# RWKV-7 chain of a two-layer hybrid block: one PSUM tile per pair for U and the state sums, the block product's four copies on ScalarE

## The chip, the cores and the metric

The kernel runs as one program on 1 core of a Trainium2 chip. The metric is the device time of one execution in microseconds (us); the time of a kernel is the median of its runs. One execution was also profiled, and all rows below come from it.

## What is computed

The reference is a two-layer block of a generator. 256 context tokens and 256 latent tokens of width 1024 go through adaLN and RMSNorm, one wide input projection, three bidirectional mixers (mLSTM, RG-LRU, RWKV-7), a gated merge, an output projection and a SwiGLU. The change concerns the RWKV-7 mixer, whose recurrence per head (16 heads of 64) and direction is:

```
def step(s, x_t):
    r_t, w_t, k_t, v_t, kap_t, kapa_t = x_t
    s_kap = jnp.einsum('bhvk,bhk->bhv', s, kap_t)
    s = s * w_t[:, :, None, :] - s_kap[..., None] * kapa_t[:, :, None, :] + v_t[..., None] * k_t[:, :, None, :]
    return s, jnp.einsum('bhvk,bhk->bhv', s, r_t)
```

## The kernel before

All large products are fp32 split into a high and a low part, three matmuls for each 128-row block, 128x512 outputs in layer 0. In each of the two layers a first stage (`weave`) runs five tasks at once: the preparation of the RWKV units (`rw_prep`, `rw_tok`, `rw_solve32` in layer 0, `rw_solve16` in layer 1), the chain (`rw_chain`), the gate of that branch, and a long list of input products (`products`, 1776 matmuls in each layer, the "products" below, tile `mm`). A second stage follows with the mLSTM heads and the RG-LRU (`ml_gates`, `ml_head`, `lru`) and the merge gates' products (line 425, also tile `mm`), then the merge, the output projection and the SwiGLU.

The order of the first stage is written out by the kernel itself when it is built. `weave` keeps a clock of its own, each task yields costs (`op("V", 290)` books 290 ns on VectorE, `took` books matmuls on TensorE, `wait` a fixed delay), and whichever task is due comes next; products are put in where no other task is due or where the recent columns are few. Inside the stage each engine executes exactly that order. The second stage is ordered by the tile scheduler. TensorE, VectorE and ScalarE run their queues strictly in the order given, so an instruction that waits holds up all behind it.

A unit is two pairs of heads (index j) times one half of the tokens; there are 8 units a layer, 8 steps of 32 tokens in each, 128 steps in all. A step (lines 1097 to 1168) is: matmuls of the old state into x (`xy`), a VectorE copy of it (`xs`, line 1106), the scaled old state (`sd`, line 1110), the matmuls for U, four copies of U into the tile UV (lines 1133 and 1136: pair j = 0 on VectorE, j = 1 on ScalarE), the matmuls of the state sums (U and V against k), the new state `Sn` (line 1153, or 1151 in a first step), and the outputs `y` (line 1163 or 1165). The next step's first matmuls wait for `Sn`. The PSUM tile `u2` is two banks of 128x512: pair j has its U in columns 0 to 127 and its state sums in columns 128 to 255 of bank j.

```
u2 = self.two()
us, sp = (u2[:, :, 128 * a:128 * a + 128].rearrange("p j (d v) -> p j d v", v=64) for a in range(2))
...
if j:
    SC.copy(UV[j][b, :, i], us[b, j])
    self.op("S", 256)
else:
    V.tensor_copy(UV[j][b, :, i], us[b, j])
    self.op("V", 290)
```

The program that the tile framework makes of this puts waits between instructions that use the same PSUM tile from two engines. `rw_solve16` (layer 1 only) inverts 32x32 triangles as two 16x16 blocks and a block product: POOL eliminates, DMAs bring the inverses back as `PT` and into `Am`, TensorE forms the two small products (tile `sm`, 16x32 and 32x16 matmuls), ScalarE writes `Z` between them, and four copies (lines 1014 and 1016, two on each engine) put the result into `Am`. The chain of a unit starts when its solve is done. `low_gemm` and `ml_head` use the same two banks outside of the first stage.

Of the kernel before, what the change touches and what calls it, by code (L numbers as in the profile page):

```python
# [22 lines left out]
S = 256  # L23
T = 512
# [189 lines left out]
class KB:  # L214
# [29 lines left out]
    def sm(self, shape):  # L244
        return self.psum("sm", shape, 2)

    def two(self):

        return self.psum("u2", [128, 2, T], 1)

    def tr(self, out, x, ident, hd):

# [303 lines left out]
        return self.pw.tile([128, T], F32, name="stage", tag="stage", bufs=SB)  # L556

    def low_gemm(self, l, h, hooks=None, mid=None, raws=None):
        ps = self.two()
        pss = [ps[:, 0], ps[:, 1]]  # L560
        self.gemm2(pss, [(l, BLK[n]) for n in ("dd", "ad")], h, hooks=hooks, mid=mid, raws=raws)
        return pss

# [397 lines left out]
    def rw_solve16(self, l, u, Am, sc1):  # L961


        nc, V, G, SC, re = self.nc, self.nc.vector, self.nc.gpsimd, self.nc.scalar, self.re
        if u:
            yield ("until", ("solve", l, u - 1))
        yield ("wait", DMW)
        N = re.tile([128, 16, 16], F32, name="N")
        nc.sync.dma_start(out=N, in_=sc1.rearrange("k x h q s t -> (k x h q) s t"))
        yield ("wait", DML)  # L970
        et = re.tile([128, 64], F32, name="et")
        for i in range(1, 15):
            w = 15 - i
            tv = et[:, 0:i * w].rearrange("p (a b) -> p a b", b=w)
            G.tensor_tensor(out=tv, in0=N[:, 0:i, i:i + 1].broadcast_to([128, i, w]), in1=N[:, i:i + 1, i + 1:16].broadcast_to([128, i, w]), op=ALU.mult)
            yield ("on", self.op("G", 280 + 2.3 * i * w) - 1500)
            G.tensor_tensor(out=N[:, 0:i, i + 1:16], in0=N[:, 0:i, i + 1:16], in1=tv, op=ALU.subtract)
            yield ("on", self.op("G", 340 + 2.1 * i * w) - 1500)
        G.memset(N.rearrange("p s t -> p (s t)")[:, 0:256:17], -1.0)
        NT = re.tile([64, 16, 16], F32, name="NT")  # L980
        G.tensor_copy(NT, N[0:64].rearrange("p s t -> p t s"))
        yield ("on", self.op("G", 900) + LAT)
        sc2 = self.dr.tile([3, 2, 2, 16, 16, 16], F32, name="sc2")
        nc.sync.dma_start(out=sc2[0:2].rearrange("k x h q s t -> (k x h q) s t"), in_=N)
        nc.sync.dma_start(out=sc2[2].rearrange("x h q s t -> (x h q) s t"), in_=NT)
        yield ("wait", DML)
        PT = re.tile([128, 16, 16], F32, name="PT")
        HJ = [(x, j, 64 * x + 32 - 32 * j) for x in range(2) for j in range(2)]
        for x, j, b in HJ:
            nc.sync.dma_start(out=PT[b:b + 16], in_=sc2[2, x, j].rearrange("q s t -> s q t"))  # L990
            for k in range(2):
                r = slice(b + 16 * k, b + 16 * k + 16)
                nc.sync.dma_start(out=Am[r, j, :, :, 16 * k:16 * k + 16].rearrange("p d c t -> p (d c) t"), in_=sc2[k, x, j].rearrange("q s t -> s q t"))
        yield ("wait", DMR)

        yield ("lock", "sm")
        ps = self.sm([128, 16, 16])
        for c in range(16):
            for x, j, b in HJ:
                self.mmul(ps[b:b + 32, c], Am[b:b + 16, j, c // 8, c % 8, 0:32], PT[b:b + 16, c])  # L1000
        yield self.took()
        Z = re.tile([128, 16, 16], F32, name="Z")
        SC.activation(out=Z, in_=ps, func=AF.Identity, scale=self.c["odd"])
        yield self.end("S", 420)
        ps = self.sm([128, 16, 16])
        for c in range(16):
            for x, j, b in HJ:
                self.mmul(ps[b:b + 16, c], Z[b:b + 32, c], Am[b:b + 32, j, c // 8, c % 8, 16:32])
        yield self.took()
        for x, j, b in HJ:  # L1010
            o = Am[b:b + 16, j, :, :, 16:32]
            p = ps[b:b + 16].rearrange("p (d c) t -> p d c t", d=2)
            if j:
                SC.copy(o, p)
            else:
                V.tensor_copy(o, p)
            self.op("VS"[j], 420)
        self.locks.discard("sm")
        self.ready[u] = max(self.free[e] for e in "VS") + LAT
        self.done.add(("solve", l, u))  # L1020

    def rw_solve32(self, l, u, Am, sc1):
# [28 lines left out]
    def rw_chain(self, l, n, ctx_out, emit):  # L1051
# [18 lines left out]
        def X(hd, j):  # L1070
            return R[hd ^ j]


        def U(hd, j):
            b = 64 * (hd ^ j) + 32 - 32 * j
            return slice(b, b + 32)
# [20 lines left out]
        for i in range(8):  # L1097
            last = s == 1 and i == 7
            y = None
            if Sp is not None:  # L1100
                for d in range(2):
                    for hd, j in HJ:
                        self.mmul(x[U(hd, j), d], kr[R[hd], j, d, i, 0:32], Sp[R[hd], j, d], start=False, stop=d == 1)
                yield self.took()
            xs = rl.tile([128, 2, 64], F32, name="xs", bufs=2)
            V.tensor_copy(xs, x)
            t = self.op("V", 288)
            if not last and Sp is not None:
                sd = rl.tile([128, 2, 2, 64], F32, name="sd")
                V.tensor_tensor(out=sd, in0=Sp, in1=PL[:, :, :, i].broadcast_to([128, 2, 2, 64]), op=ALU.mult)  # L1110
                self.op("V", 527)
            if yo:
                if "sc" in self.locks:
                    yield ("lock", "sc")
                self.locks.add("sc")
                y = self.psum("sc", [128, 2, 64], 1)
                if Sp is not None:
                    for d in range(2):
                        for hd, j in HJ:
                            self.mmul(y[Q(hd, j), d], kr[R[hd], j, d, i, 32:64], Sp[R[hd], j, d], start=d == 0, stop=False)  # L1120
                    yield self.took(0.0)
            yield ("at", t + LAT)

            u2 = self.two()
            us, sp = (u2[:, :, 128 * a:128 * a + 128].rearrange("p j (d v) -> p j d v", v=64) for a in range(2))
            for d in range(2):
                for hd, j in HJ:
                    self.mmul(us[U(hd, j), j, d], Am[U(hd, j), j, d, i, 0:32], xs[U(hd, j), d])
            yield self.took()
            for hd, j in HJ:  # L1130
                b = U(hd, j)
                if j:
                    SC.copy(UV[j][b, :, i], us[b, j])  # L1133
                    self.op("S", 256)
                else:
                    V.tensor_copy(UV[j][b, :, i], us[b, j])  # L1136
                    self.op("V", 290)
            if i < 7:
                x = tokens(i + 1)
                yield self.took(0.0)  # L1140
            yield ("at", max(self.free[e] for e in "VS") + LAT)
            Sn = None
            if not last:
                for d in range(2):
                    for j in range(2):
                        for hd in range(2):
                            self.mmul(sp[R[hd], j, d], bkT[X(hd, j), j, d, i], UV[j][X(hd, j), d, i], quads=True)
                yield self.took()
                Sn = rl.tile([128, 2, 2, 64], F32, name="Sn", bufs=2)
                if Sp is None:  # L1150
                    V.tensor_copy(Sn, sp)
                else:
                    V.tensor_tensor(out=Sn, in0=sp, in1=sd, op=ALU.add)
            snt = self.op("V", 424) + LAT
            if yo:
                for d in range(2):
                    for hd, j in HJ:
                        self.mmul(y[Q(hd, j), d], Am[X(hd, j), j, d, i, 32:64], UV[j][X(hd, j), d, i], start=Sp is None, stop=Sp is None or d == 1)
                yield self.took()

                o = Y[:, i:8 - i:7 - 2 * i] if i < 4 else (Y[:, i:6 - i:7 - 2 * i] if i < 7 else Y[:, ::-7])
                if i < 4:
                    V.tensor_copy(o, y)
                else:
                    V.tensor_tensor(out=o, in0=y, in1=o, op=ALU.add)
                self.op("V", 282)
                self.locks.discard("sc")
            yield ("at", snt)
            Sp = Sn
# [331 lines left out]
    def ml_head(self, l, hd, src, ctx_out, yd):  # L1501
# [39 lines left out]
                P[d][sb] = W  # L1541
        src = [[[0], [0, 1], [0, 1, 2], [0, 1, 2, 3]], [[0, 1], [1], [0, 1, 2, 3], [0, 1, 3]]]
        u2 = self.two()
        yp = [self.psum("xy", [128, T], 1), u2[:, 0]]
        for tb in range(t0 // 128, 4):
            num = []
            rd = m2.tile([128, 4], F32, name="rd")
            for d in range(2):
                ps = self.psum("sc", [128, 257], 1) if d else u2[:, 1, 0:257]
                lst = src[d][tb]  # L1550
                for n, sb in enumerate(lst):
                    nc.tensor.matmul(ps, P[d][sb][:, 128 * tb:128 * tb + 128], v[:, sb], start=n == 0, stop=n == len(lst) - 1)  # L1552
# [377 lines left out]
```

## Time and profile before

| | before |
|---|---|
| median of 3 runs | 2903.18 us (2895.85 to 2903.63) |
| the profiled execution | 2907.76 us, its span 2906.0 us |
| busy: PE, PEld, DVE, ACT, POOL | 92%, 71%, 60%, 44%, 21% of the span |
| mean granted TensorE clock | 0.96 |
| chain stage, layer 0 and layer 1 (first to last U matmul) | 236.4 to 760, 1871.0 to 2366 us |

PE is the matmul queue, PEld the weight loads beside it, DVE is VectorE, ACT ScalarE, SP the queue that issues most DMAs. Matmuls of the trace overlap, since their ends are modelled: two neighbours that start 0.23 us apart are each shown as 0.39 us long. A bracket behind a row gives the idle time of its engine just before and what ended it. "Issue" means that the profile shows no one that was waited for.

### The profile page before, as it was taken

What the parts mean: (1) busy time and instruction counts of PE and PEld (TensorE: products, weight loads), DVE (VectorE), ACT (ScalarE), POOL (GpSimd) and SP (SyncE); (2) the same over time, 40 slices, a digit from 0 to 9 for tenths busy, and PEclk for the clock granted to TensorE, in tenths of its full rate; (3) what the DMA queues carried; (4) which work ended last, traced back from release to release, by engine and by line L of the source; (5) the groups of instructions that cost most, each with busy time, mean ns of one, the idle gap of its engine ahead of it and who ended that gap; (6) DMA issues with size and microseconds to landing.
All of it is one profiled execution on the core that took longest, in us unless ns stands there. A gap on an engine that the chain in (4) does not pass through costs nothing. (4 is left out here: it accounts for less than half of the span.)

```text
span 2906.0 us, 75026 instructions
## 1 busy us (share of the span) xinstructions
PE 2686.3 (92%) x31560; PEld 2071.4 (71%) x31560; DVE 1730.7 (60%) x3658; ACT 1273.0 (44%) x2520; POOL 606.4 (21%) x983
## 2 busy tenths in 40 slices
PE   7998899999988999999999999999889898889998
PEld 4876666666645676677777788767667665579898
DVE  4677767775678624553333366656566557867564
ACT  4543434442366522343222255444445336755553
POOL 1056556665023100020000010222322201100000
PEclk9999989999999999999999999999999898899999
DMA  6543333433453547664554345433333344377464
GB/s 220 176 131 108 100 97 100 118 107 104 142 170 99 171 159 225 216 215 143 166 172 150 114 130 172 133 98 104 93 106 101 88 147 144 95 224 250 142 185 141
DMA packets 253715, 418.17 MB, mean 144 GB/s; under 512 B 95904, under 2 KB 145824, under 8 KB 253376
## 3 DMA queue, kind: packets, MB, share of 16 engines
q1 hardware_dynamic: 231344, 336.75, 37.9%
q10 hardware_dynamic: 22032, 76.61, 9.2%
q8 instruction: 248, 4.06, 0.6%
q14 instruction: 91, 0.75, 0.1%
HBM read 347.18 MB, written 65.04 MB: 142 GB/s over the span
## 5 line engine op out<-in xcount | busy, mean ns | idle before, releaser
L260 PE MATMUL mm<-hl,whi 128*128 128x512 f32 (+1 forms) x1184 | 460.7, 389 | 9.9 <-DVE stage L549 7.9
L260 PE MATMUL mm<-hh,wlo 128*128 128x512 f32 (+1 forms) x1184 | 458.8, 387 | 0.5 <-DVE wlo L473 0.4
L260 PE MATMUL mm<-hh,whi 128*128 128x512 f32 (+1 forms) x1184 | 459.0, 388 | 0.0
L383 DVE TENSOR_TENSOR wlo<-wraw,whi 128x512 fp32r<-128x512 f32 (+1 forms) x310 | 212.5, 689 | 281.5 <-ACT whi L382 278.9
L425 PE MATMUL mm<-hh,wlo 128*128 128x512 f32 (+1 forms) x1056 | 362.3, 345 | 18.9 <-DVE wlo L383 18.9
L425 PE MATMUL mm<-hl,whi 128*128 128x512 f32 (+1 forms) x1056 | 366.7, 347 | 5.9 <-ACT whi L382 2.5
L425 PE MATMUL mm<-hh,whi 128*128 128x512 f32 (+1 forms) x1056 | 361.0, 342 | 0.0
L382 ACT CAST whi<-wraw 128x512 fp32r<-128x512 f32 (+1 forms) x310 | 188.2, 614 | 327.9 <-PE mm L425 226.6
L473 DVE TENSOR_TENSOR wlo<-wraw,whi 128x512 fp32r<-128x512 f32 x296 | 224.9, 761 | 109.1 <-ACT whi L470 107.9
L260 PEld LDWEIGHTS mm<-hl,whi 128*128 128x128 f32 x1184 | 229.0, 193 | 59.4 <-issue 7.3
L260 PEld LDWEIGHTS mm<-hh,wlo 128*128 128x128 f32 x1184 | 228.9, 193 | 46.0 <-issue 3.0
L260 PEld LDWEIGHTS mm<-hh,whi 128*128 128x128 f32 x1184 | 229.1, 194 | 43.1 <-issue 1.5
L382 ACT CAST whi<-wx 128x512 fp32r<-128x512 f32 x212 | 128.9, 609 | 266.2 <-PE mm L425 164.1
L425 PEld LDWEIGHTS mm<-hl,whi 128*128 128x128 f32 x1056 | 202.1, 191 | 55.0 <-ACT whi L382 19.4
L470 ACT CAST whi<-wraw 128x512 fp32r<-128x512 f32 x296 | 181.6, 617 | 126.6 <-PE mm L260 76.2
L425 PEld LDWEIGHTS mm<-hh,wlo 128*128 128x128 f32 x1056 | 202.0, 192 | 48.9 <-DVE wlo L383 21.2
L383 DVE TENSOR_TENSOR wlo<-wx,whi 128x512 fp32r<-128x512 f32 x212 | 144.7, 683 | 147.9 <-ACT whi L382 145.9
L1279 POOL TENSOR_TENSOR nsq<-nsq,stage 128x256 f32<-128x256 f32 (+1 forms) x28 | 26.1, 931 | 958.8 <-ACT stage L1277 693.6
L425 PEld LDWEIGHTS mm<-hh,whi 128*128 128x128 f32 x1056 | 202.3, 192 | 23.2 <-issue 3.2
L1133 ACT COPY UV<-u 32x128 f32<-32x128 f32 x256 | 65.4, 255 | 294.5 <-DVE UV L1136 293.5
L1593 PE MATMUL mm<-ylo,whi 128*128 128x256 f32 (+1 forms) x544 | 183.4, 338 | 4.6 <-DVE ylo L383 4.5
L1593 PE MATMUL mm<-yhi,wlo 128*128 128x256 f32 (+1 forms) x544 | 179.8, 331 | 0.9 <-DVE wlo L383 0.9
(332 smaller groups left out, 5458.5 us busy)
## 6 DMA issues: line engine op xcount, KB each, us to landing
wraw<-in_wA_dram ACTq DMA_DIRECT2D x144, 512.0 KB, 3.7
wraw<-in_wA_dram SPq DMA_DIRECT2D x131, 512.0 KB, 3.7
wx<-in_wA_dram SPq DMA_DIRECT2D x81, 512.0 KB, 3.7
wx<-in_wM_dram SPq DMA_DIRECT2D x55, 512.0 KB, 3.9
wraw<-in_wM_dram SPq DMA_DIRECT2D x41, 512.0 KB, 4.1
mld<-stage SPq DMA_DIRECT2D x48, 256.0 KB, 2.9
wraw<-in_wB_dram SPq DMA_DIRECT2D x23, 512.0 KB, 3.6
pd<-stage SPq DMA_DIRECT2D x40, 256.0 KB, 3.0
```

Source lines behind the costliest of these rows:

```text
L260: self.nc.tensor.matmul(out, lhsT, rhs, start=start, stop=stop)
L382: self.nc.scalar.copy(hi[i], x[i])
L383: self.nc.vector.tensor_tensor(out=lo[i], in0=x[i], in1=hi[i].bitcast(F32), op=ALU.subtract)
L425: self.nc.tensor.matmul(ps, x[k], y[:, koff + k, t0:t0 + n], start=start and i == 0, stop=stop and i == 3 * nk - 1)
L470: self.nc.scalar.copy(hi, x)
L473: self.nc.vector.tensor_tensor(out=lo, in0=x, in1=hi.bitcast(F32), op=ALU.subtract)
L1133: SC.copy(UV[j][b, :, i], us[b, j])
L1279: (eng or self.nc.gpsimd).tensor_tensor(out=nsq, in0=nsq, in1=sq, op=ALU.add)
L1593: self.nc.tensor.matmul(ps, x[k], y[k][:, t0:t1], start=i == 0, stop=i == 3 * KC - 1)
```

## The change

`two()` now makes two tiles u0 and u1, one for each pair, of 128x4x64 in the chain; U is blocks 0 and 1 of a tile, the state sums blocks 2 and 3. The state update is one VectorE instruction for each pair (128x128) and no longer one for both (128x256), and is booked as 2 x 290 ns, not 424. The block product's four copies are all on ScalarE, booked as 4 x 360 ns. The wait that the order books for the DMAs into `Am` and `PT` ahead of the block product grows from 5000 to 6500 ns. `low_gemm` and `ml_head` take the two tiles by index.

```
-    def two(self):
-
-        return self.psum("u2", [128, 2, T], 1)
+    def two(self, shapes=((128, T), (128, T))):
+
+        return [self.psum(f"u{i}", list(x), 1) for i, x in enumerate(shapes)]
...
-        yield ("wait", DMR)
+        yield ("wait", DMR + 1500)
...
-            if j:
-                SC.copy(o, p)
-            else:
-                V.tensor_copy(o, p)
-            self.op("VS"[j], 420)
+            SC.copy(o, p)
+            self.op("S", 360)
         self.locks.discard("sm")
-        self.ready[u] = max(self.free[e] for e in "VS") + LAT
+        self.ready[u] = self.free["S"] + LAT
...
-            u2 = self.two()
-            us, sp = (u2[:, :, 128 * a:128 * a + 128].rearrange("p j (d v) -> p j d v", v=64) for a in range(2))
+            us = self.two(((128, 4, 64), (128, 4, 64)))
+            sp = [x[:, 2:4] for x in us]
...
-                    SC.copy(UV[j][b, :, i], us[b, j])
+                    SC.copy(UV[j][b, :, i], us[j][b, 0:2])
...
-                    V.tensor_copy(UV[j][b, :, i], us[b, j])
+                    V.tensor_copy(UV[j][b, :, i], us[j][b, 0:2])
...
-                if Sp is None:
-                    V.tensor_copy(Sn, sp)
-                else:
-                    V.tensor_tensor(out=Sn, in0=sp, in1=sd, op=ALU.add)
-            snt = self.op("V", 424) + LAT
+                for j in range(2):
+                    if Sp is None:
+                        V.tensor_copy(Sn[:, j], sp[j])
+                    else:
+                        V.tensor_tensor(out=Sn[:, j], in0=sp[j], in1=sd[:, j], op=ALU.add)
+                    self.op("V", 290)
+            snt = self.free["V"] + LAT
```

The new costs move the order of the whole first stage. Three places, as each engine's queue has them (name<-inputs and shape; in brackets the engines and DMA queues whose signal the instruction waits for; "x2" is the same twice).

VectorE in the second step of layer 0's chain, before:

```order
L1136 COPY UV_1481<-u_2521 32x2x64 [waits PE_49]
L1136 COPY UV_1481<-u_2521 32x2x64 [waits Activation_49]
L473 TENSOR_TENSOR wlo<-wraw,whi 128x512 [waits DMAHW2_49,Activation_49]
L1153 TENSOR_TENSOR Sn<-u_2521,sd 128x256 [waits DVE_49,PE_49]
L1163 COPY Y<-sc 128x2x64 [waits PE_49]
```

and now:

```order
L1132 COPY UV_1482<-u_2524 32x2x64 [waits PE_49]
L1132 COPY UV_1482<-u_2524 32x2x64
L473 TENSOR_TENSOR wlo<-wraw,whi 128x512 [waits DMAHW2_49,Activation_49]
L1150 TENSOR_TENSOR Sn<-u_2524,sd 128x128 [waits DVE_49,PE_49]
L1150 TENSOR_TENSOR Sn<-u_2525,sd 128x128 [waits PE_49]
L1161 COPY Y<-sc 128x2x64 [waits PE_49]
```

The second copy of U no longer waits for ScalarE, and `Sn` is two instructions. ScalarE's two copies of the step, which read `[waits DVE_49] x2` before, now have one wait, for PE.

PE where layer 0's first stage ends, before (the last products, then the transposes of `ml_gates`, line 1497, and the first mLSTM matmuls):

```order
L260 MATMUL mm<-hl,whi 128x512
L260 MATMUL mm<-hh,whi 128x512
L260 MATMUL mm<-hh,wlo 128x512
L1497 MATMUL sm<-cst,W_10941 128x36 [waits DVE_49]
L1497 MATMUL sm<-cst,W_10941 128x36 x3
L1497 MATMUL sm<-cst,W_10942 128x36 [waits DVE_49]
L1497 MATMUL sm<-cst,W_10942 128x36 x3
L1516 MATMUL sc<-cst,mvT 128x128 [waits DMAHW1_49,PE_49]
```

and now:

```order
L260 MATMUL mm<-hl,whi 128x512
L260 MATMUL mm<-hh,whi 128x512
L260 MATMUL mm<-hh,wlo 128x512
L425 MATMUL mm<-hl,whi 128x512 [waits Activation_49]
L425 MATMUL mm<-hh,whi 128x512
L425 MATMUL mm<-hh,wlo 128x512 [waits DVE_49]
```

After the last product 57 matmuls of the merge gates (line 425) now stand ahead of the transposes of `ml_gates`. Of the 1776 products of layer 0, 1648 stood ahead of the chain's last U matmuls before, and 1711 do now; in layer 1 it is 1687 before and 1702 now (of 1776). In layer 1, 72 merge-gate matmuls stood between the last product and the first mLSTM matmul, and 96 do now. Ahead of the last mLSTM or RG-LRU matmul of layer 0 stood 181 merge-gate matmuls and now 176; in layer 1 267 and now 263.

ScalarE at the first block product of layer 1, before:

```order
L470 CAST whi<-wraw 128x512 [waits PE_49]
L1003 ACTIVATE Z<-sm,cst 128x256 [waits PE_49]
L546 ACTIVATE stage<-mm,dvec 128x512 [waits DMAHW5_49,PE_49]
L1014 COPY Am<-sm 16x16x16 [waits DVE_49] x2
L470 CAST whi<-wraw 128x512 [waits DMAHW6_49]
```

and now:

```order
L470 CAST whi<-wraw 128x512 [waits DMAHW6_49]
L1002 ACTIVATE Z<-sm,cst 128x256 [waits PE_49]
L1012 COPY Am<-sm 16x16x16 [waits PE_49]
L1012 COPY Am<-sm 16x16x16 x3
L399 DMA wraw<-in_wA_dram 128x1024 [waits DMAHW1_49,DVE_49]
```

The two copies that waited for VectorE became four that wait once, for PE.

## Rows read from the trace of the kernel before

**Rows 1.** Stretches: length; PE, PEld, DVE, ACT, POOL busy (instructions); PEclk; DMA share, GB/s
```profile
240.00:795.00 555.00, 509.06 (x9912) 365.92 (x9912) 384.47 (x864) 209.70 (x468) 298.90 (x456) 0.97 0.37 106
795.00:990.00 195.00, 170.45 (x633) 99.90 (x634) 153.40 (x353) 128.09 (x229) 44.65 (x73) 0.94 0.40 130
1860.00:2366.00 506.00, 455.56 (x11112) 351.09 (x11115) 304.95 (x763) 212.57 (x491) 114.74 (x233) 0.92 0.35 97
2395.00:2570.00 175.00, 141.56 (x648) 92.80 (x649) 135.33 (x294) 116.42 (x215) 23.59 (x49) 0.85 0.44 133
```

**Rows 2.** One step's four copies (timeline: start, length), then idle before users of tile u
```profile
2006.95 0.28 DVE L1136 COPY UV<-u 32x128 f32<-32x128 f32 x1 [0.37 <-PE u L260]
2007.27 0.26 ACT L1133 COPY UV<-u 32x128 f32<-32x128 f32 x1 [3.62 <-DVE UV L1136]
2007.56 0.30 DVE L1136 COPY UV<-u 32x128 f32<-32x128 f32 x1 [0.32 <-ACT UV L1133]
2007.89 0.26 ACT L1133 COPY UV<-u 32x128 f32<-32x128 f32 x1 [0.36 <-DVE UV L1136]
...
  DVE UV L1136: 293.5, 225
  ACT UV L1133: 132.0, 236
```

**Rows 3.** PE's waits, 150 to 760 us (layer 0): total us, times, longest
```profile
PE u L260 <- ACT UV L1133: 15.8, 23, 1.7
PE xy L260 <- DVE Sn L1153: 6.9, 12, 1.3
```

**Rows 4.** PE's waits, 1780 to 2380 us (layer 1)
```profile
PE sm L260 <- DMA Am<-sc: 15.7, 13, 3.6
...
PE u L260 <- ACT UV L1133: 8.9, 17, 1.5
```

**Rows 5.** State update and output add (ns min/median/max), then one step's end on DVE
```profile
L1153 DVE TENSOR_TENSOR Sn<-u,sd x112: 412/424/427, 254.2 to 2363.9; 128x256 f32<-128x256 f32 x112
L1165 DVE TENSOR_TENSOR Y<-sc,Y x48: 278/280/292, 279.9 to 2368.2; 128x128 f32<-128x128 f32 x48
2363.88 0.42 DVE L1153 TENSOR_TENSOR Sn<-u,sd 128x256 f32<-128x256 f32 x1 [0.94 <-PE u L260]
2364.22 0.28 DVE L1165 TENSOR_TENSOR Y<-sc,Y 128x128 f32<-128x128 f32 x1
2364.41 0.68 DVE L473 TENSOR_TENSOR wlo<-wraw,whi 128x512 fp32r<-128x512 f32 x1
```

**Rows 6.** Stretches, columns as in rows 1, at two of layer 1's eight block products
```profile
1934.00:1942.00 8.00, 6.28 (x109) 4.38 (x101) 3.59 (x9) 1.34 (x3) 0.00 (x0) 0.57 0.35 111
2053.00:2068.00 15.00, 11.08 (x327) 9.76 (x325) 6.29 (x16) 3.48 (x8) 0.00 (x0) 0.54 0.35 95
```

**Rows 7.** PE timeline: last U of layer 0, the last products, the gates' transposes
```profile
760.05 0.43 PE L260 MATMUL u<-xs,Am 32*32 32x64 f32 x16
...
791.61 0.40 PE L260 MATMUL mm<-hh,whi 128*128 128x512 f32 x1
791.84 0.40 PE L260 MATMUL mm<-hh,wlo 128*128 128x512 f32 x1
...
795.82 0.64 PE L1497 MATMUL sm<-cst,W 36*128 36x36 f32 x4 [3.21 <-DVE W L1488]
```

**Rows 8.** The same of layer 1: last U, first mLSTM transposes, the gates' transposes
```profile
2365.92 0.43 PE L260 MATMUL u<-xs,Am 32*32 32x64 f32 x16
...
2393.05 0.41 PE L1516 MATMUL sc<-cst,mvT 128*128 128x128 f32 x2 [0.17 <-DMA mvT<-mld]
...
2404.97 0.64 PE L1497 MATMUL sm<-cst,W 36*128 36x36 f32 x4 [1.81 <-DVE W L1488]
```

**Rows 9.** The block product's copies by line, ns min/median/max
```profile
L1014 ACT COPY Am<-sm x16: 361/362/366, 1865.9 to 2327.8; 16x256 f32<-16x256 f32 x16
...
L1016 DVE COPY Am<-sm x16: 417/424/431, 1865.5 to 2327.3; 16x256 f32<-16x256 f32 x16
```

More of the change, by code (lines that the diff above doesn't have):

```diff
@@ L558, in low_gemm @@
     def low_gemm(self, l, h, hooks=None, mid=None, raws=None):
-        ps = self.two()
-        pss = [ps[:, 0], ps[:, 1]]
+        pss = self.two()
         self.gemm2(pss, [(l, BLK[n]) for n in ("dd", "ad")], h, hooks=hooks, mid=mid, raws=raws)
@@ L1122, in rw_chain @@
             yield ("at", t + LAT)
-            u2 = self.two()
-            us, sp = (u2[:, :, 128 * a:128 * a + 128].rearrange("p j (d v) -> p j d v", v=64) for a in range(2))
+            us = self.two(((128, 4, 64), (128, 4, 64)))
+            sp = [x[:, 2:4] for x in us]
             for d in range(2):
                 for hd, j in HJ:
-                    self.mmul(us[U(hd, j), j, d], Am[U(hd, j), j, d, i, 0:32], xs[U(hd, j), d])
+                    self.mmul(us[j][U(hd, j), d], Am[U(hd, j), j, d, i, 0:32], xs[U(hd, j), d])
             yield self.took()
@@ L1146, in rw_chain @@
                         for hd in range(2):
-                            self.mmul(sp[R[hd], j, d], bkT[X(hd, j), j, d, i], UV[j][X(hd, j), d, i], quads=True)
+                            self.mmul(sp[j][R[hd], d], bkT[X(hd, j), j, d, i], UV[j][X(hd, j), d, i], quads=True)
                 yield self.took()
                 Sn = rl.tile([128, 2, 2, 64], F32, name="Sn", bufs=2)
-                if Sp is None:
-                    V.tensor_copy(Sn, sp)
-                else:
-                    V.tensor_tensor(out=Sn, in0=sp, in1=sd, op=ALU.add)
-            snt = self.op("V", 424) + LAT
+                for j in range(2):
[5 more added lines that the diff above has]
+            snt = self.free["V"] + LAT
             if yo:
@@ L1543, in ml_head @@
         u2 = self.two()
-        yp = [self.psum("xy", [128, T], 1), u2[:, 0]]
+        yp = [self.psum("xy", [128, T], 1), u2[0]]
         for tb in range(t0 // 128, 4):
@@ L1548, in ml_head @@
             for d in range(2):
-                ps = self.psum("sc", [128, 257], 1) if d else u2[:, 1, 0:257]
+                ps = self.psum("sc", [128, 257], 1) if d else u2[1][:, 0:257]
                 lst = src[d][tb]
```

## The prediction

> **What bounds the kernel now.** I read the stretches first. [...] The products keep TensorE full and follow a fixed order, so a chain step costs time only where PE, with no product left before it, stands and waits. Shortening the chain by itself is worth nothing; what counts is PE's waits, and after them the hand-over to the mLSTM stage, whose gates need the chain's last result.
>
> So next the users of tile u. The four copies of one step run strictly in turn: VectorE at 2006.95, ScalarE at 2007.27, VectorE at 2007.56, ScalarE from 2007.89 to 2008.15, 1.20 us in all, each released by the one ahead [rows 2]. The two pairs lie in different banks and go to different tiles, so nothing of the data asks for this. Over the run ScalarE stands 293.5 us and VectorE 132.0 us for these turns [rows 2]. Of that, PE feels little: before the state sums it waits 15.8 us in layer 0 (23 times, longest 1.7) and 8.9 us in layer 1 (17 times, longest 1.5) [rows 3, 4]. Beside it stand 6.9 us for `Sn` [rows 3] and, in layer 1, 15.7 us in which the block product waits for its DMAs [rows 4].
>
> **The change part by part.**
>
> *Copies of U.* Without turns a step takes two copies of one engine, 0.28 + 0.30 = 0.58 us, and no longer 1.20 [rows 2]: 0.6 us less. The waits average 15.8 / 23 = 0.69 us in layer 0 and 8.9 / 17 = 0.52 us in layer 1 [rows 3, 4]; one that is shorter than 0.6 goes altogether, of a longer one the rest stays. The bounds are nothing and the whole 24.7 us. I take 70%, since the longest waits are nearly three times 0.6 and most of the others are below it: 11 us in layer 0, 6.5 in layer 1. In all other steps the gain is hidden under products. What is late next is `Sn`.
>
> *State update by pair.* 120 updates (112 and 8 first ones) become 240. VectorE starts a 128x128 operation out of PSUM and the next one 0.19 us later (2364.22, 2364.41), and the operation takes 0.28; so the second half ends 0.47 us after the first began, against 0.42 for the whole [rows 5]: 0.05 us more in the chain. If the two did not overlap at all it would be 2 x 0.28 - 0.42 = 0.14 us, 17 us over 120 steps, which is the upper bound; the lower one is 0, as nearly all steps have products there. I take 0.05 us on the waits for `Sn`, 12 in layer 0: some 1 us with what layer 1 adds. [...]
>
> *Longer booked wait before the block product.* It moves the matmuls of 8 solves back by up to 1.5 us, with products in front. The most is 8 x 1.5 = 12 us, the least nothing (a wait that was none before); 15.7 us came in 13 pieces of up to 3.6 us [rows 4], so I count five solves in full: 7.5 us. The chain of that unit starts as much later, covered by products.
>
> [...]
>
> *Four copies on ScalarE.* In turn they took 2 x 0.42 + 2 x 0.36 us and the hand-overs; now 4 x 0.36 = 1.45 [rows 9]. No wait of PE for them is among the large ones: 0.
>
> *Order and hand-over, layer 0.* Products leave PE every 0.23 us (791.61, 791.84) [rows 7]. 63 more of them now stand ahead of the chain's end (1711 against 1648): 14.6 us. Against that PE gets there 11 - 1 = 10 us sooner, so the chain ends 4.6 us later. The gates' second transposes came at 795.82, 36 us after the last U at 760.05, and PE had waited 3.2 us for them with no products left [rows 7]; so this path sets the start of the next stage, and that start moves 4.6 us back, to 800.4. PE isn't idle there: the last product would end at 792.1 - 10, the 57 merge-gate matmuls moved up take 57 x 0.23 = 13.2, and it stands ready at 795. That work is then missing behind: inside the mLSTM stage 176 - 57 = 119 remain of 181, so 62, or 14.4 us of PE. That stage has PE 170 and VectorE 153 of 195 us [rows 1]; neither alone bounds it, so half comes back, 7.2, between 0 and 14.4. Five more matmuls come after it: 1.2. Layer 0: + 4.6 - 7.2 + 1.2 = -1.4 us.
>
> *Layer 1.* 6.5 + 7.5 + 3 = 17 us less; 15 more products ahead of the chain's end cost at most 15 x 0.23 = 3.5. The gates' transposes at 2404.97 come 39 us after the last U at 2365.92 [rows 8], the same path, so the next stage starts 13.5 us earlier. 28 fewer merge-gate matmuls in it (167 of 195; half as wide, so I estimate 0.12 us) give half of 3.4, and four more follow it: -1.2. Layer 1: -14.7 us.
>
> Sum: -16 us. The profiled execution is 2907.76 us, 4.6 above the median of the runs shown, so I take the sum off the median: 2903.2 - 16 = **2887 us**.
>
> **The rivals.**
>
> *All of it returns.* Every U wait goes (15.8 and 8.9), 12 us for the solves, 9 of clock, and the moved products come back in full. Layer 0: 14.6 - 15.8 - 14.4 + 1.2 = -14; layer 1: -(8.9 + 12 + 9) + 3.5 - 3 = -29. 2860 us. For it: VectorE is also rid of 132 us of standing [rows 2], so that `Sn` and `xs` come sooner. Against: waits of 1.7 us hold more than the turns.
>
> *Lost at the hand-over.* The mLSTM stage is VectorE's (153 of 195 us) and gets no shorter without its 62 products; layer 0 is then + 4.6 + 1.2 = +6, and layer 1 gives 14. 2895 us, no change. For it: PE there waits for VectorE at the start [rows 7].
>
> *Slower: the next wait in line.* PE arrives sooner at the state sums, and stands for `Sn` and `xs` in place of U, as VectorE is 69% busy in layer 0 and now has 120 instructions more. If no halves of `Sn` overlap, that is up to 17 us more on VectorE, and in layer 0, where the chain's end decides, I let 2 of the 10 us remain. Then the hand-over is 12.6 us late and nothing returns, + 13.8; layer 1 yields 3 of 17 and loses 3.5 on the order. Total +14: 2917 us. It decides from the point where both layers together save less than some 10 us ahead of their chains' ends. [...] Against it: the 132 us that VectorE gets back are far more than the 6 to 17 us it has to do.
>
> *The change doesn't do what it says.* The turns could be the chip's and not the program's, and remain. In the new order ScalarE's and VectorE's copies carry no wait for one another, so I give it next to nothing; the order's shift would then cost 14.6 + 1.2 + 3.5, the solves give 7.5 back: some +12, 2915 us.
>
> **How the numbers follow.** A measurement tells 0.3% from no change, 9 us: faster is below 2894.5, slower above 2911.9. Forecast, about 2880 to 2894: 0.45. All returns, about 2860 to 2880: 0.22. Lost at the hand-over, 2895 to 2908: 0.22. Slower, with the change that does nothing: 0.11. Faster 0.67, same 0.22, slower 0.11. The range reaches from the case where nearly all returns, 2863, through the hand-over case to 2905; the slower cases and the ends stay out. The forecast's own range is 2879 to 2894.
>
> **What would show it.** Right: ScalarE's copy of U no longer released by VectorE; PE's wait for ScalarE's UV copy at about 4 us in layer 0 and 2 in layer 1; the block product's DMA wait under 9 us; merge-gate matmuls at the end of layer 0's products and the gates' transposes near 800 us; layer 1's clock above 0.92. Wrong: PE's waits for `Sn` or `xs` grown by what U lost; the mLSTM stage of layer 0 as long as before behind a later start; or stretches of half clock at new places, which the new order can bring and which I have not priced.

## The result, and the profile after

| | before | after |
|---|---|---|
| median, runs of one set | 2902.75 us (2891.81 to 2903.63, 6 runs) | 2859.83 us (2858.9 to 2865.19, 6 runs) |
| ratio | | 0.9867 [0.9854, 0.9879] |
| profiled span | 2906.0 us | 2863.5 us |

The change takes 43 us off by the medians of that set. In three later sets its ratio was 0.9879 [0.9856, 0.9901], 0.9877 [0.9858, 0.9896] and 0.9881 [0.9863, 0.99], some 36 us. The forecast had 16, and its range ended at 2863: too small a gain, in the right direction.

The page of the change, its first part (busy time and share of each engine):

```profile
PE 2669.4 (93%) x31560; PEld 2056.4 (72%) x31560; DVE 1733.0 (61%) x3762; ACT 1280.4 (45%) x2536; POOL 604.4 (21%) x983
```

Stretches of the change, columns as in [rows 1]: layer 0's chain and layer 1's.

```profile
240.00:760.00 520.00, 496.24 (x9906) 358.45 (x9897) 381.88 (x888) 207.56 (x464) 301.44 (x456) 1.00 0.39 109
1820.00:2320.00 500.00, 458.37 (x11024) 354.66 (x11022) 307.23 (x820) 223.59 (x516) 111.92 (x233) 0.92 0.37 102
```

TensorE is fuller in both chains (496 of 520 us against 509 of 555, 458 of 500 against 456 of 506): it stands 24 and 42 us where it stood 46 and 50. In layer 0 its busy time is 13 us less too, at a granted clock of 1.00 against 0.97; that part is taken up under "The clock". Layer 1's clock, 0.92, is that of before.

PE's waits in the change, 150 to 760 us (total us, times, longest), which answer to [rows 3], and 1740 to 2340 us, which answer to [rows 4]:

```profile
PE u L260 <- DVE UV L1132: 5.1, 8, 1.2
PE u L260 <- DVE xs L1102: 4.3, 7, 0.9
...
PE xy L260 <- DVE Sn L1150: 2.6, 5, 0.7
```

```profile
PE sm L260 <- issue: 19.0, 17, 2.1
PE sm L260 <- DMA Am<-sc: 9.3, 7, 3.2
```

The wait for U went from 15.8 to 5.1 us in layer 0 and that for `Sn` from 6.9 to 2.6. That for `xs` rose from 2.6 to 4.3: little took U's place. ScalarE's copy is no longer released by VectorE; the group of tile u has, in place of the two rows at the end of [rows 2], one that holds the waits for VectorE's second copy, 5.9 us of the matmuls and 18.7 of their weight loads in both layers:

```profile
  DVE UV L1132: 24.6, 44
```

The state update, twice as many operations of 0.28 us, answers to the first of [rows 5]:

```profile
L1150 DVE TENSOR_TENSOR Sn<-u,sd x224: 274/282/293, 249.6 to 2323.8; 128x128 f32<-128x128 f32 x112
```

Layer 0's hand-over, on PE's timeline (start, length), answers to [rows 7]: last U, then the gates' two transposes.

```profile
741.59 0.43 PE L260 MATMUL u<-xs,Am 32*32 32x64 f32 x16
```

```profile
774.01 0.43 PE L1495 MATMUL sm<-cst,W 36*128 36x36 f32 x4 [0.35 <-DVE W L1484]
778.91 0.44 PE L1495 MATMUL sm<-cst,W 36*128 36x36 f32 x4
```

The second of them, 37 us behind the last U as it was 36 before, comes at 778.9, not at 795.8, and not at the 800.4 that I forecast. So the chain gained more than the 63 products put ahead of its end cost.

The view that I had not read is the same list of waits for the weight loads. Their `lhsT` in the kernel is `bkT`, not U, but they come ahead of the matmuls that read U and show a wait for U's copies, 0.37 us in the load at 748.36 below. Of before, 150 to 765 us and 1740 to 2370 us:

```profile
PEld u L260 <- ACT UV L1133: 31.7, 40, 2.2
```

```profile
PEld u L260 <- ACT UV L1133: 18.0, 28, 1.9
```

and of the change:

```profile
PEld u L260 <- DVE UV L1132: 14.5, 24, 1.6
```

```profile
PEld u L260 <- DVE UV L1132: 4.2, 10, 0.6
```

The loads show 49.7 us in 68 steps where the matmuls show 24.7 in 40, and 31.0 of it is gone. But a load's wait is not all lost time. Two steps of before, the last product and the state sums behind it:

```profile
748.03 0.40 PE L260 MATMUL mm<-hh,wlo 128*128 128x512 f32 x1
748.36 0.32 PEld L260 LDWEIGHTS u<-UV,bkT 64*64 64x64 f32 x16 [0.37 <-ACT UV L1133]
748.36 0.46 PE L260 MATMUL u<-UV,bkT 64*64 64x64 f32 x16
...
751.99 0.40 PE L260 MATMUL mm<-hl,whi 128*128 128x512 f32 x1
752.75 0.46 PE L260 MATMUL u<-UV,bkT 64*64 64x64 f32 x16 [0.36 <-ACT UV L1133]
```

From start to start the first takes 0.33 us and the second 0.76. Of the 47 steps of layer 0 in which the state sums follow a product, 20 take 0.32 to 0.35 us, the least there is, and such a step loses nothing although its load shows a wait of 0.37. In the change 21 loads show a gap of 0.4 us there that the profile puts down to another row than U's copies, or to none. What the steps of layer 0 take beyond 0.33 us is 16.7 us before (19.2 in a second profile, below) and 5.7 in the change. So PE's own list, 15.8 and 5.1, has the time that U cost, and the loads' list counts some 0.36 us too much for each step.

### The profile page after: what moved, and what is told of

It reads as the page before. It is cut to its first block, busy times and chain, and to the rows that moved or that the text cites. A ratio compares the mean times of both kernels' runs of the same rounds, so it can differ in the third digit from the quotient of the medians.

```text
span 2863.5 us, 75206 instructions
## 1 busy us (share of the span) xinstructions
PE 2669.4 (93%) x31560; PEld 2056.4 (72%) x31560; DVE 1733.0 (61%) x3762; ACT 1280.4 (45%) x2536; POOL 604.4 (21%) x983
## 4 chain that ended last, share of the span: by engine, by line
PE 70%; DVE 11%; DMA 7%; issue 5%; ACT 4%; POOL 3%; SPq 1%; ACTq 0%; POOLq 0%; DVEq 0%
PE mm L425 23%; PE mm L260 20%; PE mm L1591 8%; PE sm L260 6%; DMA wraw<-in_wA_dram 3%; PE sm L1429 2%; PE u L260 2%; PE sc L260 2%; PE xy L260 2%; PE xy L1248 2%; DVE wlo L473 1%; DMA yraw<-ysc 1%; PE sm L1525 1%; PE u L1550 1%; PE u L441 1%
## 5 line engine op out<-in xcount | busy, mean ns | idle before, releaser
L1591 PE MATMUL mm<-yhi,whi 128*128 128x256 f32 (+1 forms) x544 | 179.6, 330 | 0.0
```

Source lines behind the costliest of these rows:

```text
L1591: self.nc.tensor.matmul(ps, x[k], y[k][:, t0:t1], start=i == 0, stop=i == 3 * KC - 1)
```

## The experiments

Every kernel was timed beside the kernel before, whose median was 2895.5 to 2899.7 us in the five sets. "Order held" means that in the first stages TensorE executes the same rows in the same order as in the kernel that it is compared with. In G3, G4 and H3 the second stages have the order of before too; in E1 and E2 they have an order of their own, since `ml_head` does not have the tiles of the kernel compared with, and in G6 and H1 layer 1's second stage does.

**Tiles and order apart.** Theory: the two tiles carry the gain, and the order costs or gives little.

E1, the change's tiles and updates with all bookings and the first stages' order of before (against the change; the block product's copies are as before too):

```
-        yield ("wait", DMR + 1500)
+        yield ("wait", DMR)
...
-                    self.op("V", 290)
-            snt = self.free["V"] + LAT
+            snt = self.op("V", 424) + LAT
```

> The change's two PSUM tiles and its two state updates, but with all bookings of before, so that the first stage's order on TensorE is that of before instruction by instruction; block product and booked DMA wait as before. Theory A (the turns of VectorE and ScalarE cost both the waits and the half clock that layer 0 showed at 244 to 255 and 381 to 399 us): PE's wait for U falls from 15.8 to about 5 us in layer 0, the half-clock stretches of layer 0's chain are gone, the last U of layer 0 comes some 30 us earlier than 760, and the median is about 2870 us (2862 to 2880). Theory B (the new order took the clock's falls away, the tiles only the waits): the stretch near 381 us stays at half clock, the last U comes 12 us earlier, and the median is about 2890 us.

Measured: 2868.73 us, ratio 0.9896 [0.9878, 0.9914], 29 us off the 2898.1 of its set.

E2, the opposite: before with every booking, and so the first stages' order, of the change; one tile, one update.

```
-        yield ("wait", DMR)
+        yield ("wait", DMR + 1500)
...
-            self.op("VS"[j], 420)
+            self.op("S", 360)
...
-            snt = self.op("V", 424) + LAT
+            if not last:
+                self.op("V", 290)
+                self.op("V", 290)
+            snt = self.free["V"] + LAT
```

> The new bookings and so the new order of the change, TensorE's first stage instruction by instruction, but the one PSUM tile u2, one state update, and the copies of U in turns as before; the block product's copies alternate as before. Theory A: half-clock stretches in layer 0's chain as before (20 us or more of them), the last U of layer 0 some 10 us later than 760, PE's wait for ScalarE's UV copy about 16 us there; median about 2898 us (2888 to 2906). Theory B: layer 0's chain without half clock, median about 2880 us.

Measured: 2885.6 us, ratio 0.9954 [0.9938, 0.9969], 12.5 us off, between the two cases that were expected. Both parts gain, and the tiles hold the larger one. What the order did at the hand-over, from the first and last starts of two groups of tile u (last U of layer 0; first low-rank product of layer 1):

| | last U | low-rank product | between |
|---|---|---|---|
| before, and its second profile (below) | 760.3, 751.5 | 1705.6, 1696.1 | 945.3, 944.6 |
| E1 (order of before) | 732.2 | 1680.6 | 948.4 |
| E2 (order of the change) | 762.6 | 1688.2 | 925.6 |
| the change | 741.8 | 1673.6 | 931.8 |

The products that were moved up make the chain end 10 us later (741.8 against 732.2), and 17 us (948.4 - 931.8) are missing behind it. By these single profiles they return in full. How much one profile can tell: G3 and H1 (below), the same program up to there, start the low-rank products at 1681.3 and 1673.5.

**Booked wait and the block product's copies.** E3 and again F3: the change with its booked wait back at 5000 (`DMR + 1500` to `DMR`). E4: the change with `V.tensor_copy` for j = 0 in the block product again, order held.

> The changed kernel with the booked wait ahead of the block product back at 5000 ns; layer 0 is untouched. By the prediction (7.5 us of waits and 3 us of clock) it is 8 to 10 us slower than the change: about 2869 us. Rival (the longer wait moved the matmuls and their waits together and was worth nothing): 2857 to 2863 us, PE's waits at the 16x32 matmuls within 3 us of those of the change.

> The changed kernel with the block product's four copies alternating between VectorE and ScalarE again, booked as in the change, so that TensorE's order is that of the change. By the prediction no difference (2857 to 2863 us). Rival: the 0.2 to 0.3 us of each of 8 products lies on the path of the chain's start, and VectorE has 16 more copies of 0.42 us in its queue: 2 to 5 us slower.

Measured: E3 2867.49 us, 0.9892 [0.9871, 0.9912]; E4 2858.21 us, 0.9864 [0.9847, 0.9882]. The four copies on ScalarE are worth nothing: the change has 0.9867 to 0.9881 in its own sets.

> The change with the booked wait of before the block product. Theory (the 1500 ns save what the first two medians differ by, about 8 us): 2866 to 2870 us, 6 or more above the change. Rival (they save nothing here: this kernel's block products waited no longer in its trace, 13.8 us for the DMAs and 11.9 with no releaser, against 9.3 and 19.0, and its profiled span was 2857.6): 2857 to 2863 us, within 3 of the change.

> The change again, beside its neighbours on one chip: 2858 to 2862 us. Half clock in layer 0's chain: under 17 us if the turns were its cause; anything from 0 to 31 if it comes by chance.

Measured: F3 2870.33 us, 0.9904 [0.9884, 0.9925]; the change 2858.81 us, 0.9879 [0.9856, 0.9901]. E3 stands 9 us above E4 of its set and F3 11.5 above the change of its own, 0.28 and 0.25% by the ratios; in each pair the two intervals overlap. With the wait alone added to the kernel before (G6), and with twice the addition in the change (G5):

> The kernel before with the booked wait alone lengthened by 1500 ns: one tile, one update, layer 0's order as before. If the booked wait makes up the order's whole gain of 12 us: 2882 to 2890 us. If it needs the shorter chain, or the other bookings (57 gate products moved in layer 0) make the gain: 2893 to 2903 us.

> The change with 3000 ns in place of 1500 added to the booked wait. If TensorE's waits before the block product go on falling (9 us for DMAs and 16 to 19 without a releaser are left): 2848 to 2854 us. If 1500 has taken what there was, or the later chain gives it back: 2857 to 2866 us.

Measured: G6 2888.69 us, 0.9973 [0.996, 0.9986]; G5 2860.03 us, 0.9883 [0.987, 0.9897]. By the three comparisons the first 1500 ns are worth some 8 us, the next 1500 nothing. The forecast's 7.5 us has the size, but the waits don't show it where I put it: in layer 1 the DMA wait fell from 15.7 [rows 4] to 9.3, while the same matmuls' wait with no releaser, 19.0 in the change, was 9.1 before. Where these us come from stays open.

**What in the tiles.** Is it the length of the copies in a row, or what the turns do to the two engines? E5 is E1 with all four copies of U on ScalarE, order held:

```
-                    V.tensor_copy(UV[j][b, :, i], us[j][b, 0:2])
+                    SC.copy(UV[j][b, :, i], us[j][b, 0:2])
```

> Two tiles for U and the state sums and an update by pair, in the order of before, but all four copies of U on ScalarE, so that they stand in a row again (about 4 x 0.26 us, in place of two beside two) while VectorE has 256 operations fewer and never waits for ScalarE's turn. Theory A (what the tiles save is the time by which U is late): U waits of 12 us or more in layer 0 again, and most of the 29 us lost: 2880 to 2890 us. Theory B (what they save is VectorE's standing, so that the other operands come sooner): the time stays at 2863 to 2872 us, or falls.

Measured: 2871.9 us, 0.991 [0.9891, 0.9929]. The time is that of theory B, and PE waited 0.4 us for U in layer 0 where E1 waited 8.6: a row of four on one engine, 1.04 us of copies, doesn't make U late here, so the length of the row alone was not the cost. That leaves the turns. So G3 leaves out the tiles: before, with that word changed and nothing else, order held.

```
-                    V.tensor_copy(UV[j][b, :, i], us[b, j])
+                    SC.copy(UV[j][b, :, i], us[b, j])
```

> The kernel before, one tile and one update, with one word changed: all four copies of U on ScalarE. No engine is then handed the tile in turn, the four copies still stand in a row, and TensorE's order is that of before. Theory T (the turns cost what stands in the two engines' queues at each hand-over, and that is all the two tiles remove): 2866 to 2878 us, with U waits of 5 us or less in layer 0. Rival R (the two tiles themselves do it, here, in the gates or in low_gemm; or the update by pair does): 2890 us or more.

Measured: 2862.2 us, 0.9885 [0.987, 0.9901]. One word, with one tile and one update, gives 34.6 us, as much as the tiles with their update by pair (29; the intervals overlap). The weight loads' waits in G3, 150 to 765 us:

```profile
PEld u L260 <- ACT UV L1133: 16.1, 30, 1.2
```

Half of the 31.7; from start to start the state sums lose 5.6 us in layer 0, not 16.7. H3 does it on the fuller engine: `SC.copy` to `V.tensor_copy` for the other pair, one tile, order held.

> The kernel before, one tile, with all four copies of U on VectorE: no turns, but 256 more operations on the engine that has the longest queue. If the changes of engine were the cost: 2862 to 2880 us, with U waits under 12 us in layer 0. If VectorE's load is it: 2896 us or more, with waits for U and Sn that grow.

Measured: 2880.42 us, 0.9943 [0.9926, 0.9961]; its loads wait nearly as long as before,

```profile
PEld u L260 <- DVE UV L1133: 28.1, 34, 2.0
```

and its state sums still lose 14.7 us in layer 0. It gains 15 us even so, with 128 operations more on VectorE for each layer; PE's wait for `Sn` fell from 6.9 us to 0.8. Neither expected case holds whole: the time is that of the first, the waits for U are not (14.1 us by PE's list). So the changes of engine cost by themselves. G3 takes 256 operations from VectorE and H3 gives it as many more; halfway between their gains lie 25 us, an estimate of the turns alone, and E1, which moves no copy, has 29 with the by-pair update in it. That the 20 us between G3 and H3 are VectorE's queue is argued and not tested by itself. How a turn costs more than the copies shows in a step of before, on ScalarE's and then VectorE's timeline:

```profile
341.01 0.62 ACT L727 ACTIVATE th<-th 128x512 f32<-128x512 f32 x1
341.53 0.80 ACT L730 ACTIVATE kt<-at,dvec 128x512 f32<-128x512 f32 x1
342.36 0.26 ACT L1133 COPY UV<-u 32x128 f32<-32x128 f32 x1
342.98 0.25 ACT L1133 COPY UV<-u 32x128 f32<-32x128 f32 x1 [0.36 <-DVE UV L1136]
```

```profile
341.07 0.28 DVE L1136 COPY UV<-u 32x128 f32<-32x128 f32 x1
342.64 0.30 DVE L1136 COPY UV<-u 32x128 f32<-32x128 f32 x1 [1.29 <-ACT UV L1133]
342.98 0.98 DVE L732 TENSOR_TENSOR kt<-kt,kr 128x512 f32<-128x512 f32 x1
```

VectorE copied the first quarter at 341.07; ScalarE had two operations of 512 columns ahead of its own, came at 342.36, and VectorE stood 1.29 us with its next work behind the third copy. The step took 2.2 us from the first copy to the last, not the 1.20 of [rows 2]. Over layer 0's 64 steps, from the end of U's matmuls to that of the last copy (PE's, VectorE's and ScalarE's timelines), the median is 1.72 us before, 1.20 in the change, 1.14 in G3 and E5, 1.28 in H3.

G4 tests the update by pair alone: before, `Sn` written in two instructions from the one tile, order held.

```
-                if Sp is None:
-                    V.tensor_copy(Sn, sp)
-                else:
-                    V.tensor_tensor(out=Sn, in0=sp, in1=sd, op=ALU.add)
+                for j in range(2):
+                    if Sp is None:
+                        V.tensor_copy(Sn[:, j], sp[:, j])
+                    else:
+                        V.tensor_tensor(out=Sn[:, j], in0=sp[:, j], in1=sd[:, j], op=ALU.add)
```

> The kernel before with the state update an operation per pair, from the one tile: 120 operations more, turns kept. My prediction's theory (about 0.05 us each, hidden): within 4 us of before, 2893 to 2903. The prediction's slower rival (no overlap, 17 us on VectorE that the chain feels): 2908 us or more, with longer waits for Sn. If the update by pair shortens the chain by itself (products of the next step start on one pair's half): 2888 us or less.

Measured: 2901.01 us, 1.0021 [1.001, 1.0032]: it costs 3 to 9 us. VectorE's busy time is 1739.1 us, 8.4 more than the 1730.7 of before. PE's wait for `Sn` in layer 0 did not grow (5.3 us against 6.9), so where the time goes is not shown. The price fits most of what E5 lacks against G3.

**The clock.** Layer 0's chain had three stretches of half clock before, 30.7 us in all, and none in the change, whose granted clock there was 1.00. F1 is the kernel before in a second profile.

> The kernel before, profiled a second time, for the stretches at half clock in layer 0's chain (31 us in its first profile, 0 to 20 in those of the kernels without the turns). If the turns bring them about: 17 us or more of them again, near 250, 390 or 600 us. If they come by chance in any execution: as likely near 0. Span 2890 to 2908 us either way.

Its span was 2889.4 us. The stretch from 381 to 399 us in the first profile of before (columns as in [rows 1]), and in the second:

```profile
381.00:399.00 18.00, 17.59 (x276) 13.22 (x265) 7.23 (x19) 4.06 (x9) 10.81 (x19) 0.53 0.21 62
```

```profile
381.00:399.00 18.00, 15.83 (x399) 11.35 (x392) 8.82 (x25) 4.88 (x13) 14.36 (x27) 1.00 0.16 49
```

The same program ran 276 matmuls there at a granted clock of 0.53, and 399 at 1.00, and the last U came at 751.5, not 760.3. Over its whole chain of layer 0 the second profile has 3.4 us of half clock, the first 30.7. H1 (below), which has no turns, has 24 us of it in its chain of layer 0, this stretch among them:

```profile
506.00:516.00 10.00, 10.00 (x120) 7.00 (x123) 3.32 (x7) 3.94 (x10) 5.35 (x11) 0.50 0.29 83
```

So the stretches don't need the turns and don't follow from them; they come and go from one execution to the next. By these two profiles some 9 us of the 42.5 between the two first spans may be theirs. The medians of several runs differ by some 36 us all the same.

**A version that beats both.** H1 is G3 with the booked wait of 6500; H2 is the change with its four copies of U on ScalarE; I1 is E2 with that word, that is G3 in the change's order.

> The kernel before with two edits of one place each: all four copies of U on ScalarE, and 1500 ns more of booked wait; one tile, one update, everything else as before. If the two add (34.6 and 8 us): 2851 to 2858 us, some 5 below the change. If the shorter chain has already taken what the booked wait gave: 2859 to 2865 us.

> The change with its four copies of U on ScalarE as well; two tiles, updates by pair, TensorE's order that of the change. If VectorE's copies still made U late there (5 us of waits in layer 0): 2852 to 2857 us. If, as between the two kernels with the order held, ScalarE's row of four gives nothing or loses 3: 2858 to 2866 us.

> The change a third time, beside the two kernels that may beat it, on one chip: 2857 to 2862 us, as in its two earlier sets of runs.

Measured: H1 2861.17 us, 0.9885 [0.9865, 0.9904]; H2 2862.8 us, 0.9885 [0.9861, 0.991]; the change 2859.83 us, 0.9877 [0.9858, 0.9896]. None beats it: the booked wait adds nothing to G3, which is the second of the two cases expected, and which does not fit the 8 us above.

> One tile and one update as before, all four copies of U on ScalarE, and TensorE's order that of the change in every row (its booked wait and its other bookings). If the gates' products moved up in layer 0 are worth their 5 us and the update by pair costs its 6: 2848 to 2855 us, under the change. If order and chain take the same time twice, as with the booked wait alone: 2857 to 2865 us.

> The change once more, on the chip of the kernel that may beat it: 2857 to 2862 us, as in its three earlier sets of runs.

Measured: I1 2853.19 us, 0.9835 [0.9816, 0.9853]; the change, on the same chip, 2866.48 us, 0.9881 [0.9863, 0.99]: above the time that was expected for it, beside a kernel before of 2899.7, with the ratio of the other sets. I1 is the fastest kernel here: the change's order in the first stages, one tile, one update, no turns.

## Why the prediction was wrong

**Copies of U: the term that failed.** The step that failed is "what counts is PE's waits": it took the waits for U as all that the tiles can give back, with "The bounds are nothing and the whole 24.7 us". The waits themselves fell as forecast: 17.5 us were to go, and PE's list lost 10.7 in layer 0 and 8.1 in layer 1 (15.8 to 5.1, 8.9 to 0.8). But the tiles give 29 us with the by-pair update in it, and G3 34.6 without. With the order held, the chain from first to last U shrank by more than its waits for U:

| first to last U | layer 0 | layer 1 |
|---|---|---|
| before, and its second profile | 523.9, 515.0 | 495.1, 492.1 |
| E1 | 497.6 | 479.0 |
| G3 | 498.3 | 480.0 |

That is 17 to 26 us in layer 0 and 12 to 16 in layer 1, where I had 11 and 6.5. What the rest is stays open. No one wait holds it: in H3 it is `Sn`, in G3 it is not, and half clock differs between executions (30.7 and 3.4 us in the two profiles of before). The 0.6 us of a step was near the median (1.72 to 1.20 us) but taken from one in which nothing else was queued. "What is late next is `Sn`" did not come: PE's wait for it fell to 2.6 us. The turns alone don't explain that, since it stays at 7.9 in G3, without turns and with one update, and is 5.3 in G4, with turns and the update by pair. PE's waits for `Sn` in layer 0, in G3, G4 and H3:

```profile
PE xy L260 <- DVE Sn L1153: 7.9, 11, 1.5
```

```profile
PE xy L260 <- DVE Sn L1154: 5.3, 12, 1.3
```

```profile
PE xy L260 <- DVE Sn L1153: 0.8, 1, 0.8
```

**By place.** Layer 0 was to give 1.4 us and layer 1 14.7. Up to layer 1's first low-rank product the change gains 32 us (1705.6 to 1673.6), or 22 against the second profile of before; from there to the end 10.5 or 3.

**VectorE's standing, misread.** The 132.0 us at the end of [rows 2] are those of all users of tile u: 24.7 are PE's and 49.7 the weight loads', and VectorE's own are

```profile
DVE UV L1136 <- ACT UV L1133: 57.6, 128, 1.3
```

ScalarE's 293.5 us are not all for the turns either, since its first copy cannot come before U: in the change it waits 206.0 us for PE at that place. The rivals were weighed with 132; 57.6 is still more than the 6 to 17 us held against it.

**State update by pair.** 1 us forecast between 0 and 17; G4 measures 3 to 9. VectorE is 8.4 us longer busy for 120 instructions, 0.07 us each, close to the 0.05 of the start-to-start row; by the time, the cover of products that I counted on did not hold.

**Order and hand-over.** "so half comes back" was too little: by the profiles above all 14.4 us and some more. For layer 0 the new order meant +14.6 - 7.2 + 1.2 = 8.6 us in my sum; E1, which has the order of before, starts layer 1's low-rank products at 1680.6, and E3, F3 and the change, with the new one, at 1672.2, 1678.4 and 1673.6: 2 to 8 us of gain. One program's profiles differ by 8 there (G3, H1), so the sign rests on all three, and on E2 and I1, which are faster than before and G3. I had taken the half because neither PE nor VectorE alone bounds the mLSTM stage; but those products would have had to run behind the chain in any case, on an engine that is 93% busy. I also overlooked that `ml_head` has two tiles now: from the first to the last transpose of `hT`, E1's stage takes 142.7 us (787.5 to 930.2), against 162.3 in G3 with one tile (788.9 to 951.2), yet layer 1's products start 948.4 and 947.9 us behind the last U. That gain is given back whole; that it is for the reason above, since the same products remain to be run, is argued.

**Longer booked wait.** 7.5 us forecast; 9 and 11.5 by E3 and F3, 8 by G6, nothing beside G3. The size was right in the change; the waits do not confirm the mechanism, and in G6 and H1 the order of layer 1's second stage moved as well.

**Clock.** No run shows the 3 us that the sum takes off layer 1 for the clock at the block products [rows 6]: its chain was granted 0.92 before [rows 1] and 0.92 in the change. What I had not priced, the half clock of layer 0, comes with and without the turns: 30.7 and 3.4 us in two profiles of before, none in the first profile of the change, 24 us in H1.

**Four copies on ScalarE.** 0 forecast, 0 measured.

**The rivals.** "All of it returns" has the time, 2860, and it is right on most of U's waits and on the moved products. But of its 12 us for the solves some 8 came, of its 9 of clock, which no run shows either, nothing, and layer 0 gave 22 to 32 us where it had 14: that its sum meets the time is luck. "Slower" had a true price in it, the update by pair, 3 to 9 of its 17 us, which the turns outweigh several times.

By the runs the sum reads, in ratios: tiles with the by-pair update -1.0%, order with the booked wait another -0.15 to -0.3% on top of them, -0.46% by itself and -0.5% from G3 to I1. How it divides between the booked wait and the hand-over differs from pair to pair by about as much as the intervals are wide, and stays open.

## What to carry to other kernels

Where a tile is handed between two engines in turn, each turn cost here what stood in the queue of the engine that was next, and the engine that waited stood with all its own work, 1.29 us in the step at 341 us; putting the whole tile on the emptier engine was worth as much as splitting it (34.6 us against 29), for one word, without the extra instructions that the split brings. The matmul's wait for a late operand is no upper bound for what such an edit gives: here the waits for U fell by the forecast 17.5 us or a little more, and the tiles gave 29. Check a list of waits by the starts of the rows, since the weight loads' list counted a gap, 0.37 us at 748.36, in steps that lose nothing. And read in a group's row of waits who it is that waits. Products that must run in any case came back in full here when they were moved, on a TensorE that is 93% busy.

## What the runs showed that I had not expected

Half clock in a chain full of products differs between executions of one program: between 381 and 399 us it was 0.53 of full speed in one and 1.00 in another, and the last U of the first came 9 us later. A comparison of two single profiles has to be read with that much doubt.
